# One buffer set for weight blocks and left sums in the first MLP product, with the next pair's blocks asked for at the pair's begin

## The chip, the cores and the metric

The kernel runs on one core of one Trainium2 chip. The metric is device time in microseconds (us) for one execution; the number given for the kernel before is the median of three runs. TensorE is called PE here, VectorE DVE, ScalarE ACT, GpSimd POOL, and SyncE, which only issues DMAs here, SP.

## The reference

The reference is one layer of a streaming encoder on 1024 prompt rows and 64 sample rows: RMSNorm, one input projection, sparse attention and band attention side by side, gates, an output projection and a residual, then an MLP. Only the MLP's first product is touched by the change:

```python
D_MODEL = 1024
SEQ = 1024
DEC_SEQ = 64
D_FF = 4 * D_MODEL

# x: the residual stream, (rows, 1024); w_up (1024, 4096); w_down (4096, 1024)
h = jnp.square(jax.nn.relu(rmsnorm(x, g) @ w_up))
x = x + h @ w_down
```

Rows are 1088 in all, taken as two halves of 544. Everything is float32; a product is made of three matmuls, `hi*hi + hi*lo + lo*hi`, on operands split into a high and a low part.

## The kernel before

The first product, squared ReLU of x times `w_up`, runs over 16 *pairs* of 128 columns of `w_up` (4096 columns in 16 times 256). Each pair is a two-by-two block product done with seven block products in place of eight (Strassen's way, in Winograd's form): the weight blocks are called 11, 12, 21 and 22 (512 x 128 each), the x side was prepared as the split operands T1, T2, T3, T4, B11, B21 and B22, which stay in memory. One block product (`product`) is 24 matmuls 128x272 into two halves of a PSUM tile: 4 slices of the contraction, 2 halves of the rows, 3 matmuls. PE, 24 matmuls at a time, is what the loop is built to feed.

`sums(p)` (L1008) asks for the four blocks of pair p by four DMAs on SP (L1012) and makes four sums of them on DVE: L1014 S1 = 21 + 22, L1015 S3 = 11 - 21 in place, L1016 S2 = S1 - 11 in place, L1017 S4 = 12 - S2 in place. Block 22 stays as it is. `operand` (L1020) splits one such sum: the high part by a copy on ACT (L123), the low part by a subtraction on DVE (L1024). `columns_of` (L647) loads and splits a block of `w_up` that needs no sum (a tile named raw, DMA L652, low part L146). High and low parts live in a ring of five.

The loop `for p in range(NPAIR)` (L1079) does for pair p the products, in program order: T2 with S2 into PSUM tile pf; for the first eight pairs, B11 of pair p + 8 into pa (`first_product`); T1 with S1 into pe; T3 with S3 into pg; for the first eight pairs, B21 of pair p + 8 on top of pa (`second_product`); B22 with S4 on top of pe; T4 with block 22 on top of pg. So pairs 0 to 7 do seven products, and pairs 8 to 15, whose first two were made ahead, do five. Each of pf, pa, pe and pg is one buffer.

DVE reads the PSUM tiles between products: L1087 u from pf; L1096 v from pe after T1 (B22 on pe waits for it); L1103 v from pg after T3 (T4 on pg waits for it); L1109 from pe after B22; L1116 from pg after T4. The results v, u and so on are squared on ACT (L977, L978) and sent out by ACT (L980). Four *left sums* of the results, for the second product, are made on DVE too: L1113 s1, L1118 s2, L1120 in place, L1122 in a12, the block A12 of h that SP reads back from memory (L1100). `sums_out` (L984) sends them out on ACT (L986) one pair later.

All the blocks, the a12 tile and the left sums s1 and s2 are [128, 544] tiles of the pool `up`, by tags: three buffers each for the tags 11, 12, 21 and 22, and two for S1. The a12 tile uses tag 22, s1 uses tag 11 and s2 tag 12. So tag 22's three buffers serve two tiles a pair, block 22 and a12. Before the loop, `quarter(k)` (L1038) prepares a quarter of x's operands with the same tags; its DVE lines are L1044 to L1046 and L1053.

What sets the order: each engine takes its instructions strictly in its own order. A scheduler puts the program's instructions on each engine's queue with the help of simulated times and the program's order as priority; a tile of a pool can be written again when the readers of the buffer's last tile are done. A DMA also waits for the one that used its completion semaphore eight DMAs earlier. In the program, `sums(p + 1)` is called after T1 and L1096 of pair p, `sums_out` after the low part of T1's operand.

Of the kernel before, what the change touches and what calls it, by code (L numbers as in the profile page):

```python
# [10 lines left out]
F32 = mybir.dt.float32  # L11
# [7 lines left out]
P = 128  # L19
# [19 lines left out]
HALF = T // 2  # L39
# [5 lines left out]
def kernel(  # L45
# [8 lines left out]
    nc = tc.nc  # L54
# [26 lines left out]
    def bank(tag, n=512):  # L81
        pool, bufs = banks[tag]
        return pool.tile([P, n], F32, tag=tag, name=tag, bufs=bufs)
# [5 lines left out]
    def open_pool(name, side="left", **reuse):  # L89
        st = ExitStack()  # L90
        p = st.enter_context(tc.tile_pool(name=name, bufs=1, side=side, **reuse))
        pools[name] = st
        return p
# [28 lines left out]
    def copy(out, in_):  # L122
        return nc.scalar.activation(out, in_, AF.Copy)  # L123

    last = {}
# [17 lines left out]
    def split(raw, hi, lo, lo_on_vector=False):  # L143
        copy(hi, raw)
        if lo_on_vector:
            nc.vector.tensor_sub(lo, raw, hi)  # L146
        else:
            nc.gpsimd.tensor_sub(lo, raw, hi)  # L148
# [482 lines left out]
    for g in range(0, EARLY, 4):  # L631
        ws = []
        for k in range(KB):
            raw = pj.tile([P, 512], F32, tag="wraw", name="wraw", bufs=2)
            nc.sync.dma_start(raw, w_in[k * P:(k + 1) * P, C_G + g * P:C_G + g * P + 512])
            hi = pj.tile([P, 512], F32R, tag="whi", name="whi", bufs=11)
            lo = pj.tile([P, 512], F32R, tag="wlo", name="wlo", bufs=11)
# [152 lines left out]
    for mix in "ba":  # L790
        oT[mix] = cp.tile([P, 4, 2, T], F32R, name=f"oT_{mix}")
        for k in range(4):
            for c0, n in CHUNKS:
                raw = cp.tile([P, 384], F32, tag="oraw", name="oraw", bufs=2)[:, :n]
                nc.sync.dma_start(raw, o_dram[mix][k * P:(k + 1) * P, c0:c0 + n])
                hi = oT[mix][:, k, 0, c0:c0 + n]
# [114 lines left out]
    for rows_here in (first_rows, second_rows):  # L911
        for g in range(0, D, 256):
            ws = []
            for k in range(0, KB, 2):
                raw = ring.tile([P, 2, 256], F32, tag="raw", name="raw", bufs=3)
                hi = ring.tile([P, 2, 256], F32R, tag="hi", name="hi", bufs=RING)
                lo = ring.tile([P, 2, 256], F32R, tag="lo", name="lo", bufs=RING)
# [16 lines left out]
    NPAIR = DFF // 256  # L934
# [3 lines left out]
    def product(ps, w, x, opens):  # L938
        for k in range(4):
            for c in range(2):  # L940
                cols = slice(c * HALF // 2, (c + 1) * HALF // 2)
                last = three(ps[:, c * 512:c * 512 + HALF // 2], [(w[k], (xops[x][:, k, 0, cols], xops[x][:, k, 1, cols]))],
                             opens and k == 0, k == 3, not opens)
        return last
# [21 lines left out]
    up = open_pool("up", "right", reuse_waits="tile")  # L966

    def temp(tag, n):
        return hp.tile([P, 2, HALF // 2], F32, tag=tag, name=tag, bufs=n)
# [14 lines left out]
    def sums_out():  # L984
        for p, nm, t in made:
            nc.scalar.dma_start(h_dram[p][BLOCK[nm]][:, :512], t)  # L986
        made.clear()
# [3 lines left out]
    def first_product(p, tag):  # L991
        if p not in begun:
            begin(p, tag)
        ps = begun.pop(p)
        c1 = temp("c1", NEAR + 2)
        copy(c1, halves(ps))
        firsts[p] = ps, c1
# [5 lines left out]
        firsts[p] = c1  # L1003

    def block(nm):
        return up.tile([P, HALF], F32, tag=nm, name=nm, bufs=2 if nm == "s1" else 3)

    def sums(p):  # L1008
        a = {}
        for nm, r, c in (("21", 0, P), ("22", 512, P), ("11", 0, 0), ("12", 512, 0)):  # L1010
            a[nm] = block(nm)[:, :512].rearrange("p (k c) -> p k c", k=4)
            nc.sync.dma_start(a[nm], w_up[r:r + 512, p * 256 + c:p * 256 + c + P].rearrange("(k p) c -> p k c", p=P))  # L1012
        s1 = block("s1")[:, :512].rearrange("p (k c) -> p k c", k=4)
        nc.vector.tensor_add(s1, a["21"], a["22"])  # L1014
        nc.vector.tensor_sub(a["21"], a["11"], a["21"])  # L1015
        nc.vector.tensor_sub(a["11"], s1, a["11"])  # L1016
        nc.vector.tensor_sub(a["12"], a["12"], a["11"])  # L1017
        return {"S1": s1, "S2": a["11"], "S3": a["21"], "S4": a["12"], "A22": a["22"]}

    def operand(src):  # L1020
        hi = ring.tile([P, 4, P], F32R, tag="hi", name="hi", bufs=RING)
        lo = ring.tile([P, 4, P], F32R, tag="lo", name="lo", bufs=RING)
        copy(hi, src)
        last["low"] = nc.vector.tensor_sub(lo, src, hi)  # L1024
        return [(hi[:, k], lo[:, k]) for k in range(4)]

    sources = sums(0)
# [38 lines left out]
    def first_operands():  # L1066
        h, w = (xo.tile([P, 4, 2, HALF], F32R, tag=f"x{nm}_of_x", name=f"first_{nm}", bufs=1) for nm in ("B11", "B21"))
        for k in range(4):
            pair = []
            for t, src, on_vector in ((h, h_dram[k][BLOCK["A11"]][:, :512], True),  # L1070
                                      (w, w_down[k * 256 + P:(k + 1) * 256, :512], True)):
                raw = ring.tile([P, 512], F32, tag="raw", name="raw", bufs=3)
                nc.sync.dma_start(raw, src)
                hi, lo = t[:, k, 0, :512], t[:, k, 1, :512]
                split(raw, hi, lo, lo_on_vector=on_vector)
                pair.append((hi, lo))
            first_ops.append(pair)

    for p in range(NPAIR):  # L1079
        ahead = p + NEAR < NPAIR  # L1080
        if p == NEAR + 2:
            first_operands()
        src = sources
        x6 = bank("pf", 1024)
        product(x6, operand(src["S2"]), "T2", True)
        u = firsts.pop(p)
        nc.vector.tensor_add(u, halves(x6), u)  # L1087
        if ahead:
            first_product(p + NEAR, "pa")
        x5 = bank("pe", 1024)  # L1090
        product(x5, operand(src["S1"]), "T1", True)

        with tc.issue_after(last["low"].ins):
            sums_out()
        v = temp("h", 5)
        nc.vector.tensor_add(v, halves(x5), u)  # L1096
        if p + 1 < NPAIR:
            sources = sums(p + 1)
        a12 = block("22")[:, :512]
        nc.sync.dma_start(a12, h_dram[p][BLOCK["A12"]][:, :512])  # L1100
        x7 = bank("pg", 1024)
        product(x7, operand(src["S3"]), "T3", True)
        nc.vector.tensor_add(v, halves(x7), v)  # L1103
        square_out(p, "A21", v, v)
        if ahead:
            second_product(p + NEAR)
        product(x5, operand(src["S4"]), "B22", False)
        w = temp("h", 5)
        nc.vector.tensor_add(w, halves(x5), u)  # L1109
        square_out(p, "A22", w, w)  # L1110
        a11, a21, a22 = (flat_of(t)[:, :512] for t in (u, v, w))
        s1, s2 = block("11")[:, :512], block("12")[:, :512]
        nc.vector.tensor_add(s1, a21, a22)  # L1113
        made.append((p, "S1", s1))
        product(x7, operand(src["A22"]), "T4", False)
        nc.vector.tensor_add(u, halves(x7), u)  # L1116
        square_out(p, "A11", u, u)
        nc.vector.tensor_sub(s2, s1, a11)  # L1118
        made.append((p, "S2", s2))
        nc.vector.tensor_sub(a21, a11, a21)  # L1120
        made.append((p, "S3", a21))
        nc.vector.tensor_sub(a12, a12, s2)  # L1122
        made.append((p, "S4", a12))
# [117 lines left out]
    for g in range(QUAD):  # L1241
        few = few_operands(g)
        for nm in ("P1", "P2", "P5", "P6", "P3", "P7", "P4"):
# [13 lines left out]
            for k in range(4):  # L1257
                p = 4 * g + k
# [75 lines left out]
```

## Time and profile before

| | |
|---|---|
| median of 3 runs | 1754.68 us (1754.44 to 1754.83) |
| the profiled execution's own time | 1754.13 us |
| its span, first to last instruction | 1752.0 us |
| mean granted clock of PE | 0.995 of full |
| PE busy | 1715.1 us, 98% of the span |
| DVE / ACT / POOL busy | 1200.9 / 957.5 / 478.9 us |
| first MLP product (pairs 0 to 15) | from 1104.94 to 1409.32 us of the span |

The profile is one execution. Its views give, for any stretch, how long each engine was busy, what each idle stretch before an instruction was waiting for, and when each instruction began. A wait is put down to the releaser that came last. PE's matmuls overlap, so PE's busy share says little of small losses; the time from one product's first matmul to the next one's says more.

### The profile page before, as it was taken

To read this page: it belongs to the slowest core of one execution; us is meant where nothing else is said; L and a number is where in the kernel's file an instruction comes from. 1 tells how busy PE (TensorE), PEld (TensorE's weight loads), DVE (VectorE), ACT (ScalarE), POOL (GpSimd) and SP (SyncE) were. 2 spreads that over 40 slices of the span, in tenths; PEclk is the share of its full clock that TensorE was granted. 3 is DMA by queue.
4 is the path that set the end of the run, shared out by engine and by line. 5 is a ranking of instruction groups with operands and counts; after the bars stand their busy time and mean duration, and the time that the engine had idled before them with its cause. 6 is when DMAs were issued, how large, how long until landed. Compare 5 with 4: busy or idle time off the path is not lost.

```text
span 1752.0 us, 30862 instructions
## 1 busy us (share of the span) xinstructions
PE 1715.1 (98%) x10540; PEld 1554.2 (89%) x10540; DVE 1200.9 (69%) x2765; ACT 957.5 (55%) x1994; POOL 478.9 (27%) x549
## 2 busy tenths in 40 slices
PE   8999999999999999999999999999999999999999
PEld 6877888877999999999999999999989988888887
DVE  6877799994457777774354446855577758878787
ACT  5785889722357777775443346644444446443430
POOL 2252432544423333332343444000000011310122
PEclk9999999999999999999999999999999999999999
DMA  5032475454667876654544458654566589665643
GB/s 177 5 89 102 144 200 152 144 167 152 179 165 195 194 170 160 164 133 145 170 141 147 168 173 270 203 169 152 171 198 200 169 282 317 191 205 145 199 126 102
DMA packets 277197, 294.97 MB, mean 168 GB/s; under 512 B 39792, under 2 KB 201584, under 8 KB 277040
## 3 DMA queue, kind: packets, MB, share of 16 engines
q1 hardware_dynamic: 248064, 257.61, 50.7%
q10 hardware_dynamic: 28976, 35.40, 5.7%
q8 instruction: 83, 1.36, 0.3%
q14 instruction: 74, 0.61, 0.1%
HBM read 199.85 MB, written 93.08 MB: 167 GB/s over the span
## 4 chain that ended last, share of the span: by engine, by line
PE 66%; DVE 6%; DMA 4%; issue 2%; ACT 2%; POOL 1%; ACTq 0%; SPq 0%; DVEq 0%; POOLq 0%
PE acc L154 7%; PE acc L156 7%; PE acc L155 7%; PE x L156 5%; PE x L155 5%; PE x L154 5%; PE pt L699 4%; PE po L715 2%; PE s L162 2%; PE po L714 2%; PE s L163 2%; PE few L1253 1%; PE pe L155 1%; PE pe L154 1%; PE pe L156 1%
## 5 line engine op out<-in xcount | busy, mean ns | idle before, releaser
L155 PE MATMUL x<-lo,hi 128*128 128x512 f32 x432 | 168.6, 390 | 0.7 <-POOL lo L148 0.7
L156 PE MATMUL x<-hi,lo 128*128 128x512 f32 x432 | 166.8, 391 | 0.0
L154 PE MATMUL x<-hi 128*128 128x512 f32 x432 | 164.2, 392 | 0.0
L148 POOL TENSOR_TENSOR lo<-wr,hi 128x512 fp32r<-128x512 f32 x15 | 34.5, 2300 | 467.3 <-ACT hi L123 467.3
L148 POOL TENSOR_TENSOR lo<-raw,hi 128x512 fp32r<-128x512 f32 x88 | 117.4, 1344 | 156.8 <-ACT hi L123 156.1
L123 ACT ACTIVATE hi<-raw 128x512 fp32r<-128x512 f32 x104 | 64.2, 626 | 90.5 <-PE acc L155 21.1
L711 DVE TENSOR_TENSOR pl<-pt,ph 128x512 fp32r<-128x512 f32 (+4 forms) x184 | 96.6, 545 | 19.5 <-ACT ph L123 18.9
L536 ACT ACTIVATE nth<-work,cand 128x768 bf16<-128x768 f32 (+2 forms) x93 | 96.6, 1038 | 20.6 <-DVE cand L553 15.3
L146 DVE TENSOR_TENSOR lo<-hr,hi 128x512 fp32r<-128x512 f32 x108 | 81.6, 757 | 27.4 <-ACT hi L123 27.1
L123 ACT ACTIVATE ph<-pt 128x512 fp32r<-128x512 f32 (+4 forms) x184 | 81.6, 483 | 32.5 <-PE pt L699 25.6
L155 PEld LDWEIGHTS x<-lo,hi 128*128 128x128 f32 x432 | 81.1, 188 | 19.2 <-POOL lo L148 1.1
L156 PEld LDWEIGHTS x<-hi,lo 128*128 128x128 f32 x432 | 81.1, 188 | 17.9
L154 PEld LDWEIGHTS x<-hi 128*128 128x128 f32 x432 | 81.1, 188 | 17.5
L154 PE MATMUL acc<-xnT,hi 128*128 128x384 f32 (+1 forms) x288 | 95.4, 331 | 0.0
L156 PE MATMUL acc<-xnT,lo 128*128 128x384 f32 (+1 forms) x288 | 94.3, 327 | 0.0
L155 PE MATMUL acc<-xnT,hi 128*128 128x384 f32 (+1 forms) x288 | 94.3, 327 | 0.0
L686 POOL TENSOR_SCALAR mw<-mw,sm 128x640 f32<-128x640 f32 (+1 forms) x64 | 56.7, 886 | 131.9 <-DVE sm L685 131.8
L154 PE MATMUL wide<-whi,xnT 128*128 128x512 f32 x224 | 89.5, 405 | 1.7 <-DVE work_s L366 1.7
L156 PE MATMUL wide<-whi,xnT 128*128 128x512 f32 x224 | 90.2, 403 | 0.0
L155 PE MATMUL wide<-wlo,xnT 128*128 128x512 f32 x224 | 89.8, 401 | 0.0
L714 PE MATMUL po<-ph,vhl 128*128 128x256 f32 (+2 forms) x336 | 86.0, 274 | 0.4 <-ACT ph L123 0.4
L715 PE MATMUL po<-pl,vhl 128*128 128x256 f32 (+2 forms) x336 | 85.9, 286 | 0.6 <-DVE pl L711 0.6
(671 smaller groups left out, 5973.7 us busy)
## 6 DMA issues: line engine op xcount, KB each, us to landing
hr<-h SPq DMA_DIRECT2D x108, 256.0 KB, 3.7
wr<-in_w_down_dram SPq DMA_DIRECT2D x76, 256.0 KB, 4.0
wraw<-in_w_in_dram SPq DMA_DIRECT2D x56, 256.0 KB, 2.9
h<-h ACTq DMA_DIRECT2D x32, 272.0 KB, 3.1
raw<-in_w_out_dram SPq DMA_DIRECT2D x32, 256.0 KB, 3.1
raw<-in_w_up_dram SPq DMA_DIRECT2D x32, 256.0 KB, 3.7
out_dram<-t SPq DMA_DIRECT2D x24, 256.0 KB, 2.4
g_dram<-gate SPq DMA_DIRECT2D x32, 192.0 KB, 3.4
```

Source lines behind the costliest of these rows:

```text
L123: return nc.scalar.activation(out, in_, AF.Copy)
L146: nc.vector.tensor_sub(lo, raw, hi)
L148: nc.gpsimd.tensor_sub(lo, raw, hi)
L154: nc.tensor.matmul(out, sh, mh, start=(opens and i == 0), stop=False, skip_group_check=resumes)
L155: nc.tensor.matmul(out, sh, ml, start=False, stop=False, skip_group_check=resumes)
L156: last = nc.tensor.matmul(out, sl, mh, start=False, stop=(closes and i == n - 1), skip_group_check=resumes)
L536: nc.scalar.activation(sign[:, :w.shape[1]], w, AF.Sign, bias=against, scale=-1.0, accum_out=col(cnt, j))
L686: nc.gpsimd.tensor_scalar(m[:rows, :n], m[:rows, :n], sm[:rows, 6:7], 1.0, op0=ALU.mult, op1=ALU.mult)
L699: nc.tensor.transpose(ps[:krows, oo:oo + qrows], m[:qrows, kc:kc + krows], ident[:qrows, :qrows])
L711: nc.vector.tensor_sub(pl[:kr, a:b], ps[:kr, a:b], ph[:kr, a:b])
L714: nc.tensor.matmul(dst, vhl[:krows, vt, :], ph[:krows, oo:oo + width], start=(idx == 0), stop=False)
L715: nc.tensor.matmul(dst, vhl[:krows, vt, :], pl[:krows, oo:oo + width], start=False, stop=(idx == n - 1))
```

## The change

`block` now gives all its tiles from one tag, "block", with 14 buffers, as many as the five tags had together; a12, s1 and s2 come from there too. `sums(p + 1)`, with its four DMAs on SP and its four sums on DVE, is called at pair p's begin, ahead of T2's product, in place of after L1096. The low part of `operand` goes through `split`, the same two instructions under another line number (L146 in place of L1024), and `sums_out()` is no longer told to come behind the low part of T1's operand. The number of matmuls, DMAs and bytes is the same.

```diff
     def block(nm):
-        return up.tile([P, HALF], F32, tag=nm, name=nm, bufs=2 if nm == "s1" else 3)
+        return up.tile([P, HALF], F32, tag="block", name=nm, bufs=14)
...
     def operand(src):
         hi = ring.tile([P, 4, P], F32R, tag="hi", name="hi", bufs=RING)
         lo = ring.tile([P, 4, P], F32R, tag="lo", name="lo", bufs=RING)
-        copy(hi, src)
-        last["low"] = nc.vector.tensor_sub(lo, src, hi)
+        split(src, hi, lo, lo_on_vector=True)
...
         src = sources
+        if p + 1 < NPAIR:
+            sources = sums(p + 1)
         x6 = bank("pf", 1024)
         product(x6, operand(src["S2"]), "T2", True)
...
-        with tc.issue_after(last["low"].ins):
-            sums_out()
+        sums_out()
         v = temp("h", 5)
         nc.vector.tensor_add(v, halves(x5), u)
-        if p + 1 < NPAIR:
-            sources = sums(p + 1)
-        a12 = block("22")[:, :512]
+        a12 = block("a12")[:, :512]
         nc.sync.dma_start(a12, h_dram[p][BLOCK["A12"]][:, :512])
```

Line numbers behind the change shift a little: L1087 becomes L1088, L1100 L1098, L1103 L1101, L1109 L1107, L1113 L1111, L1116 L1114, L1118 L1116, L1120 L1118 and L1122 L1120; L1012 to L1017 and L1096 stay.

DVE's order in pair 3, from u of the pair to v's second sum. Before (the numbers in the names count tiles: 12_15052 and 22_15048 are pair 3's sums, 11_15301 and 12_15303 pair 4's, 21_15548, 22_15550 and s1_15556 pair 5's):

```order
L1087 TENSOR_TENSOR c1_13990<-pf_15199,c1_13990 128x544
L1122 TENSOR_TENSOR 22_15059<-22_15059,12_15162 128x512
L1024 TENSOR_TENSOR lo_15380<-12_15052,hi_15379 128x512
L1017 TENSOR_TENSOR 12_15303<-12_15303,11_15301 128x512
L1024 TENSOR_TENSOR lo_15416<-22_15048,hi_15415 128x512
L1096 TENSOR_TENSOR h_15295<-pe_15262,c1_13990 128x544
L1024 TENSOR_TENSOR lo_15452<-11_15301,hi_15451 128x512
L1014 TENSOR_TENSOR s1_15556<-21_15548,22_15550 128x512
L1103 TENSOR_TENSOR h_15295<-pg_15312,h_15295 128x544
```

The same stretch of DVE now (12_14954 and 22_14950 are pair 3's, the names from 15199 to 15207 pair 4's):

```order
L1088 TENSOR_TENSOR c1_13990<-pf_15212,c1_13990 128x544
L1120 TENSOR_TENSOR a12_15059<-a12_15059,12_15162 128x512
L1014 TENSOR_TENSOR s1_15207<-21_15199,22_15201 128x512
L1015 TENSOR_TENSOR 21_15199<-11_15203,21_15199 128x512
L146 TENSOR_TENSOR lo_15380<-12_14954,hi_15379 128x512
L146 TENSOR_TENSOR lo_15416<-22_14950,hi_15415 128x512
L1016 TENSOR_TENSOR 11_15203<-s1_15207,11_15203 128x512
L1096 TENSOR_TENSOR h_15308<-pe_15275,c1_13990 128x544
L1017 TENSOR_TENSOR 12_15205<-12_15205,11_15203 128x512
L146 TENSOR_TENSOR lo_15465<-11_15203,hi_15464 128x512
L1101 TENSOR_TENSOR h_15308<-pg_15312,h_15308 128x544
```

L1014, for pair 5, stood directly ahead of the row that frees pg. Now all four sums in the stretch are pair 4's, and seven rows stand between L1014 and that row.

SP's order in the early pairs, where each row asks for a tile (raw is a block for B11 or B21, the second number of a name ahead of `<-` again a tile's). Before, in pairs 3 and 4 (22_15550, 11_15552 and 12_15554 are pair 5's, 21_16050 is pair 7's):

```order
L1100 DMA 22_15310<-h3_79 128x512
L1012 DMA 22_15550<-in_w_up_dram 128x4x128
L652 DMA raw_15847<-in_w_up_dram 128x4x128
L1012 DMA 21_16050<-in_w_up_dram 128x4x128
L1012 DMA 11_15552<-in_w_up_dram 128x4x128
L1012 DMA 12_15554<-in_w_up_dram 128x4x128
```

Now, in pair 3 (the names from 15199 to 15205 are pair 4's):

```order
L652 DMA raw_15745<-in_w_up_dram 128x4x128
L1012 DMA 21_15199<-in_w_up_dram 128x4x128
L1012 DMA 22_15201<-in_w_up_dram 128x4x128
L1012 DMA 11_15203<-in_w_up_dram 128x4x128
L1012 DMA 12_15205<-in_w_up_dram 128x4x128
L1098 DMA a12_15310<-h3_79 128x512
```

The four blocks of a pair now stand together, ahead of a12, for the pair that comes next. Before, they were asked for apart and two to four pairs ahead, and block 22 stood behind a12.

DVE's order in the late pairs, here the rows between u and v's second sum of pair 10 before (16927, 16925 and s1_16929 are pair 11's):

```order
L1087 TENSOR_TENSOR c1_15009<-pf_16856,c1_15009 128x544
L1024 TENSOR_TENSOR lo_17042<-11_16925,hi_17041 128x512
L1118 TENSOR_TENSOR 12_16785<-11_16784,c1_14758 128x512
L1120 TENSOR_TENSOR h_16701<-c1_14758,h_16701 128x512
L1096 TENSOR_TENSOR h_16919<-pe_16886,c1_15009 128x544
L1122 TENSOR_TENSOR 22_16716<-22_16716,12_16785 128x512
L1024 TENSOR_TENSOR lo_17072<-s1_16929,hi_17071 128x512
L1017 TENSOR_TENSOR 12_16927<-12_16927,11_16925 128x512
L1103 TENSOR_TENSOR h_16919<-pg_16936,h_16919 128x544
```

and of the same pair now (16856 to 16864 are pair 11's):

```order
L1088 TENSOR_TENSOR c1_15022<-pf_16869,c1_15022 128x544
L1120 TENSOR_TENSOR a12_16716<-a12_16716,12_16785 128x512
L1096 TENSOR_TENSOR h_16932<-pe_16899,c1_15022 128x544
L1014 TENSOR_TENSOR s1_16864<-21_16856,22_16858 128x512
L1015 TENSOR_TENSOR 21_16856<-11_16860,21_16856 128x512
L1016 TENSOR_TENSOR 11_16860<-s1_16864,11_16860 128x512
L1101 TENSOR_TENSOR h_16932<-pg_16936,h_16932 128x544
```

Here three sums of the next pair (L1014 to L1016) have come between v's two sums. PE's order in these pairs changes with it: before, a first part of the next pair's T2 stood ahead of B22 or T4 of a pair; now a pair's five products stand one behind the other.

## Rows read from the trace of the kernel before

**Rows 1.** The page's first part: busy us, share of the span, instructions.

```profile
PE 1715.1 (98%) x10540; PEld 1554.2 (89%) x10540; DVE 1200.9 (69%) x2765; ACT 957.5 (55%) x1994; POOL 478.9 (27%) x549
```

**Rows 2.** Stretches: from:to, length, busy us by engine, granted clock, DMA share, GB/s.

```profile
1104.94:1128.40 23.46, 21.62 (x170) 21.18 (x169) 17.53 (x28) 14.11 (x24) 0.00 (x0) 1.00 0.51 156
1128.40:1149.46 21.06, 21.06 (x171) 21.06 (x169) 11.55 (x20) 8.64 (x15) 0.00 (x0) 1.00 0.53 168
1149.46:1170.51 21.05, 21.05 (x170) 21.05 (x169) 12.66 (x20) 9.11 (x16) 0.00 (x0) 1.00 0.54 174
1170.51:1283.57 113.06, 107.16 (x843) 105.64 (x842) 64.26 (x101) 48.72 (x82) 0.00 (x0) 1.00 0.53 170
1283.57:1299.50 15.93, 13.05 (x91) 12.64 (x90) 14.16 (x23) 9.08 (x17) 0.00 (x0) 0.90 0.68 222
1299.50:1409.30 109.80, 109.80 (x873) 109.80 (x872) 76.40 (x122) 48.52 (x78) 0.00 (x0) 1.00 0.55 176
```

**Rows 3.** PE's waits, 1100 to 1412 us: who waited for whom, total, times, longest.

```profile
PE pg L154 <- DVE h L1103: 4.5, 5, 1.7
PE pf L156 <- DVE lo L1024: 1.8, 1, 1.8
...
PE pa L154 <- ACT c L123: 1.4, 1, 1.4
PE pf L154 <- ACT hi L123: 1.1, 1, 1.1
```

**Rows 4.** PE's timeline, pair 3: start, length, what, [idle before, releaser].

```profile
1188.43 0.29 PE L156 MATMUL pe<-xB_of_x,lo 128*128 128x272 f32 x1
1189.37 0.39 PE L154 MATMUL pg<-xT_of_x,hi 128*128 128x272 f32 x1 [0.65 <-DVE h L1103]
```

**Rows 5.** DVE's timeline in the same place.

```profile
1183.34 0.68 DVE L1024 TENSOR_TENSOR lo<-11_15301,hi 128x512 fp32r<-128x512 f32 x1
1187.99 0.69 DVE L1014 TENSOR_TENSOR s<-21_15548,22_15550 128x512 f32<-128x512 f32 x1 [3.97 <-DMA 22_15550<-in_w_up_dram]
1188.60 0.72 DVE L1103 TENSOR_TENSOR h<-pg,h 128x544 f32<-128x544 f32 x1
```

**Rows 6.** SP's timeline in the same place.

```profile
1183.77 0.37 SPq L1012 DMA_DIRECT2D 22_15550<-in_w_up_dram  x1
```

**Rows 7.** SP's waits, 1100 to 1412 us, columns as in rows 3.

```profile
SPq L1012 <- DVE lo L1024: 51.5, 14, 6.3
```

**Rows 8.** DMAs by tile, 1180 to 1300 us: queue, count, KB, us to landing.

```profile
22_15550<-in_w_up_dram SPq DMA_DIRECT2D x1, 256.0 KB, 4.1
...
11_15803<-in_w_up_dram SPq DMA_DIRECT2D x1, 256.0 KB, 6.1
12_15805<-in_w_up_dram SPq DMA_DIRECT2D x1, 256.0 KB, 7.0
22_16052<-in_w_up_dram SPq DMA_DIRECT2D x1, 256.0 KB, 2.9
```

**Rows 9.** Timelines of DVE, ACT and PE in pair 5.

```profile
1222.98 0.69 DVE L1015 TENSOR_TENSOR 21_15799<-11_15803,21_15799 128x512 f32<-128x512 f32 x1 [4.64 <-DMA 11_15803<-in_w_up_dram]
...
1226.24 0.33 ACTq L986 DMA_DIRECT2D h<-h  x1
...
1227.80 0.39 PE L154 MATMUL pa<-xB_of_x,hi 128*128 128x272 f32 x1 [1.36 <-ACT c L123]
```

**Rows 10.** PE's timeline at the seam of pairs 8 and 9.

```profile
1296.13 0.44 PE L156 MATMUL pf<-xT_of_x,lo 128*128 128x272 f32 x1 [1.83 <-DVE lo L1024]
...
1299.77 0.29 PE L154 MATMUL pe<-xB_of_x,hi 128*128 128x272 f32 x1
```

**Rows 11.** DVE's timeline in a late pair.

```profile
1303.78 0.69 DVE L1014 TENSOR_TENSOR s<-21_16703,22_16705 128x512 f32<-128x512 f32 x1 [4.03 <-DMA 22_16705<-in_w_up_dram]
```

**Rows 12.** Timelines of DVE and PE at the loop's start.

```profile
1107.71 0.71 DVE L1046 TENSOR_TENSOR 22_14425<-22_14425,11_14421 128x544 f32<-128x544 f32 x1
...
1109.17 0.39 PE L154 MATMUL pf<-xT_of_x,hi 128*128 128x272 f32 x1 [1.79 <-ACT xT_of_x L123]
```

## The prediction, made before the changed kernel was run

> **What bounds the kernel now.** I began with the page: PE is busy 98% of the span [rows 1], so a faster DVE or DMA gives nothing by itself; only places count where PE itself stands still. Next I cut the changed loop into stretches, at the first matmul of a pair's T2 [rows 2]. Pairs 1 and 2 take 21.06 and 21.05 us and PE's busy time fills them: 168 matmuls in 21.055 us, 0.1253 us each, is what a pair costs that never waits. The reader is to set the other rows against that. Pair 0 took 23.46 us, 2.4 us too much. Pairs 3 to 7 took 113.06 us where 5 x 21.055 = 105.28 would do: 7.8 us too much. In the late part, the 90 matmuls from 1283.57 to 1299.77 [rows 2, 10] took 16.20 us in place of 90 x 0.1253 = 11.28: 4.9 us too much. The rest, 1299.50 to 1409.30, is full. So 7.8 + 4.9 = 12.7 us are lost in the loop behind pair 0, and 2.4 in pair 0. No more than about 15 us can be had here.
>
> The third view is PE's waits over the loop [rows 3]. The commonest by far is T4's first matmul, which waits for DVE's second sum of v (L1103, which frees pg): 5 times, 4.5 us, once in each of pairs 3 to 7. Three single waits follow: a copy of pa on ACT (1.4), a high part on ACT (1.1) and a low part on DVE (1.8). The timelines tell what stands behind each. In pair 3, DVE ended a low part at about 1184.0 and stood still for 3.97 us until block 22 of pair 5 had landed, since L1014 is next in its order; L1103, whose input had long been there, came only at 1188.60 [rows 5], and PE lost 0.65 us at T4 [rows 4]. A wait costs PE more than it shows: from 1188.43 to 1189.37 are 0.94 us between two starts that would be 0.13 apart, and the first matmul behind a wait takes 0.39 in place of 0.29. With both, pair 3's price is some 0.9 us.
>
> Why was block 22 late? SP asked for it at 1183.77 [rows 6] and it took 4.1 us [rows 8]. SP had waited for a low part on DVE that frees a buffer: 51.5 us over 14 such requests [rows 7]. So the chain is a loop: tag 22's three buffers serve block 22 and a12, the load is asked for when DVE has read the old tile, and DVE then waits for the load with PE's release behind it. The wait for pa in pair 5 is the same kind one step on: DVE stood 4.64 us for block 11, so the left sums of the pair before came late; ACT's issue of the one from L1120 went out only at 1226.24, and the copy of pa behind it on ACT let PE go at 1227.80, 1.36 us late [rows 9].
>
> In the seam of pairs 8 and 9 two waits follow one another, the second 1.83 us at 1296.13. Behind it PE's granted clock falls: 0.90 over that stretch, 1.00 in all others [rows 2]. From 1296.13 to 1299.77 are 16 matmuls in 3.64 us, where 2.0 would do, at starts 0.23 apart, about the lower of the two levels, 1.2 GHz. So 1.6 of the 4.9 us is the clock's.
>
> **The change part by part.** *One tag with 14 buffers.* The memory is the same, and so is the number of DMAs and matmuls; what goes is the rule that block 22 and a12 share three buffers. A pair uses eight tiles (four blocks, S1, a12, s1, s2), so 14 buffers are 1.75 pairs' worth. The instructions cost what they cost. The gain is the lost time that hangs on late blocks.
>
> *Loads and sums at the pair's begin.* Per pair, SP issues four loads for the next pair one behind the other, each 0.37 us [rows 6], ahead of a12. By my following of the semaphores, the second raw load ahead of them waits for DVE at the end of the pair before, so the four are asked for between 1.5 and 5 us into the pair; the last, block 12, waits for a left sum's output. They land between 4.5 and 12 us into it, by landings of 2.9 (alone) to 7.0 us (fourth in a row) [rows 8]. In pairs 1 to 7 L1014 and L1015 therefore still wait on DVE, about to +5.5 and +8 us, and perhaps L1017 up to +12. But what stands behind them has time: pg is full at 4 x 3.01 = 12.0 us (T2, B11, T1, T3), T4 begins at 6 x 3.01 = 18.1 us, and L1101 is 0.72 us long [rows 5]. Between them lie 6.0 us of B21 and B22, which hide a wait of up to some 5 us. The other waiter, B22 at 15.1 us, needs L1096 and one low part, both behind L1015 only; 7 us of cover. So I cost the waits that stay at nothing; if a load came at +18, the price would be that of before, 0.4 to 1.7 us a pair [rows 3]. The seven pairs' 7.8 us go. The left sums now stand ahead of L1014 on DVE, so the wait for pa in pair 5, which is part of these 7.8, goes too.
>
> *The late pairs.* In pairs 8 to 15 all loads can be asked for a pair ahead, since only half as many raw loads stand on SP. What is worse there: T2 of the next pair no longer stands ahead of T4, and L1101 has only B22's 3.0 us between the end of T3 (+9.0) and the start of T4 (+12.1). L1096 can start at T1's end (+6.0); behind it L1014, L1015 and L1016 take three times 0.61 (pitch from L1014 to L1103 [rows 5]) and end at about +8.7, before T3 does. L1101 then runs from +9.1 to +9.8: 2.3 us to spare. DVE was busy 76.40 of 109.80 us in the late pairs [rows 2], 70%, and its work there stays the same. So no wait is added and the 4.9 us of the seam go, with the clock's 1.6 among them, since the clock fell only behind those waits.
>
> *Low part's line, sums_out.* The same instructions; 0 us. ACT's order of outputs moves a little; ACT was busy 48.72 of 113.06 us [rows 2], and an output issue that waits on ACT is priced by the pair-5 wait, 1.4 us at most, once.
>
> *The loop's start.* Here L1014 of pair 1 comes two rows ahead of L1046 of the last quarter, and PE's 1.79 us wait in pair 0's T2 hangs on L1046 by way of an ACT copy [rows 12]. One more row of 0.61 us on that chain: +0.6. Ends: -2.4 (the shared tag asks for the quarter's tiles earlier and pair 0 loses nothing), and +4.0 if L1014 has to wait there as long as it did in a late pair, 4.03 us [rows 11]. I take +0.6, because block 22 is asked for some 4 us before L1014's turn, which is about the longest landing of that block that is shown [rows 8].
>
> *A remainder.* A new order of some 500 instructions on DVE and ACT [rows 2] will have some wait that I did not find; from 0 to 3.7 us (1.05 + 1.83 and their restarts, the largest that stood in one place). I take one like pair 3's, 0.9 us.
>
> Sum: -7.8 - 4.9 + 0.6 + 0.9 = -11.2 us. From the profiled execution's 1754.13 that is 1742.9; it lies 0.55 us under the median of 1754.68, so against the median 1743.5.
>
> **The rule that speaks against it.** PE's T4 wait comes five times in a row, pair by pair [rows 3]. The Trainium skill, page "Perfetto Trace Analysis", section "Identifying Performance Opportunities", says that the same gap repeating on the engine that should be full can mean that there is not enough memory for the next tile (buffer count, tile sizes). By that rule a change that adds no buffer leaves the gap, and the time would be 1754.7. The rows point at the division, not the total: SP waited for one tag while 11 other buffers of the pool were not asked. I weigh it as the third rival.
>
> **The rivals.**
> 1. *The wait moves but half of it stays.* Pairs 1 to 7 ask for blocks only in the pair before their use; if block 12 lands beyond +16 or so, T4 or the next T2's operand (S2, which needs L1016) waits. For it: landings of 6 to 7 us when several are asked for in a row [rows 8]. Against: 5 to 6 us of cover. Price: half of 7.8 stays and a start worse by 2, about 1748 (1746 to 1751). On this bears the Trainium skill, "DMA: Bandwidth & Descriptors", section "Issuing engines are not separate DMA queues": transfers run on the same 16 engines and interleave, whoever starts them. The trace agrees, 2.9 us for a load alone and 7.0 for the fourth in a row; by it block 12 comes at +12 and not at +8, still inside the cover.
> 2. *Slower: the late pairs lose their cover.* If L1014 of a late pair waits 4.03 us as it once did [rows 11], from +6.7 on, L1016 ends at +12.5 and L1101 at +13.3 in place of at most 12.0; T4 is 1.3 us late and restarts, 1.6 us, in each of eight pairs: 13 us. It decides from the point where block 22 lands later than about +9 us in the pair in which it is summed. With the start's worst (+4), the time is 1743.5 + 13 + 3 = 1759 (1758.2 to 1762); alone it gives 1756. Against: these loads are asked for a pair ahead.
> 3. *It doesn't do what it says.* The shared set comes free no earlier, because a12, s1 and s2 hold their buffers until their outputs have landed; the same waits come back, about 1754 (1751.2 to 1758.2).
>
> **How the numbers follow.** A measurement of this kernel can tell about 0.2%, 3.5 us. Forecast (1739.5 to 1746): 0.56. Rival 1 (1746 to 1751): 0.18. Rival 3 with the mild form of rival 2: 0.14. Rival 2 in full: 0.12. The likeliest gives 1743.5. Below the forecast lies only the start's gain, 1754.7 - 12.7 - 2.4 = 1739.6. The upper end takes in rival 1 and the upper edge of the unknown start, and a little of rival 3: 1752.5. Outside are about 0.2. Faster by over 0.2% (under 1751.2): 0.74; within: 0.14; slower: 0.12.
>
> **What would show it.** Right: the stretches of pairs 1 to 7 are all 21.06 us long; no wait of PE for L1101 is left; the granted clock is 1.00 at pairs 8 and 9; DVE still shows waits of L1014 and L1015 for blocks in pairs 1 to 7, harmless. Rival 1: T4 or T2 waits in the pairs from 1 to 7 behind L1017 or a low part. Rival 2: T4 waits for L1101 eight times from pair 8 on, each behind a DMA. Rival 3: SP's waits for DVE in L1012 as long as before. Wrong at the start: pair 0's stretch over 24.1 us. The whole argument falls if the time changes outside the stretch from some 1080 us to the loop's end.

## The result

The changed kernel took 1738.4 us (median of 6 runs, 1736.8 to 1742.7), the kernel before beside it 1754.5 us (6 runs, 1752.9 to 1754.8): a ratio of 0.9913, 95% interval 0.9901 to 0.9926, so 0.74 to 0.99% faster. The forecast was 1743.5 us with a range from 1739.5 to 1752.5; the time lies 1.1 us below the range.

The page of the changed kernel, first part, to be set against [rows 1]; its span is 1738.0 us, the execution's own time 1739.8 us:

```profile
PE 1709.3 (98%) x10540; PEld 1551.3 (89%) x10540; DVE 1199.3 (69%) x2765; ACT 956.4 (55%) x1994; POOL 481.4 (28%) x549
```

No engine got less work: the instructions are as many, DVE's, ACT's and POOL's busy times differ by 1.1 to 2.5 us, and PE's is 5.8 us lower. The stretches of the loop, cut as in [rows 2], tell where the time went (length, busy us of PE, weight loads, DVE, ACT and POOL, granted clock, DMA share, GB/s):

```profile
1102.98:1125.43 22.45, 21.51 (x170) 21.16 (x169) 15.85 (x26) 13.37 (x23) 0.00 (x0) 1.00 0.32 101
1125.43:1146.48 21.05, 21.05 (x170) 21.05 (x169) 12.81 (x21) 9.84 (x16) 0.00 (x0) 1.00 0.54 178
1146.48:1167.54 21.06, 21.06 (x171) 21.06 (x169) 12.91 (x21) 9.63 (x16) 0.00 (x0) 1.00 0.55 179
1167.54:1272.81 105.27, 105.27 (x843) 105.27 (x842) 66.40 (x105) 50.36 (x85) 0.00 (x0) 1.00 0.56 184
1272.81:1287.87 15.06, 15.06 (x122) 15.06 (x121) 12.92 (x21) 8.48 (x15) 0.00 (x0) 1.00 0.88 282
1287.87:1393.37 105.50, 105.50 (x843) 105.50 (x842) 76.76 (x120) 44.52 (x73) 0.00 (x0) 1.00 0.56 180
```

From pair 1 on PE's busy time fills every row, and the clock is 1.00 in the seam of pairs 8 and 9, where it was 0.90. Pairs 3 to 7 take 105.27 us, five times the 21.05 of a pair that never waits; they took 113.06. All waits of PE that are left from 1040 to 1396 us are two, both ahead of pair 0's end; compare [rows 3]:

```profile
PE pg L154 <- ACT c L123: 1.5, 1, 1.5
PE pf L154 <- ACT xT_of_x L123: 0.9, 1, 0.9
```

DVE in pair 5 of the changed kernel, which answers to [rows 5] and [rows 9], shows that it still waits for its blocks (start, length, what, idle time before it and its releaser):

```profile
1218.67 0.69 DVE L1014 TENSOR_TENSOR s<-21_15701,22_15703 128x512 f32<-128x512 f32 x1 [4.15 <-DMA 22_15703<-in_w_up_dram]
1220.49 0.69 DVE L1015 TENSOR_TENSOR 21_15701<-11_15705,21_15701 128x512 f32<-128x512 f32 x1 [1.13 <-DMA 11_15705<-in_w_up_dram]
...
1224.74 0.71 DVE L1101 TENSOR_TENSOR h<-pg,h 128x544 f32<-128x544 f32 x1
```

And PE at the same place:

```profile
1227.56 0.29 PE L156 MATMUL pe<-xB_of_x,lo 128*128 128x272 f32 x1
1227.68 0.29 PE L154 MATMUL pg<-xT_of_x,hi 128*128 128x272 f32 x1
```

L1014 stood for 4.15 us, as long as before. But it did so from 4.9 to 9.0 us in a pair of 21, and the row that frees pg ended at 1225.45, 2.2 us before T4 wanted it: the two starts of PE are 0.12 us apart. So the wait was not removed; it was moved to a place where it is hidden.

### The profile page after: what moved, and what is told of

The parts are those of the page before. It is cut to its first block, busy times and chain, and to the rows that moved or that the text cites. A ratio compares the mean times of both kernels' runs of the same rounds, so it can differ in the third digit from the quotient of the medians.

```text
span 1738.0 us, 30914 instructions
## 1 busy us (share of the span) xinstructions
PE 1709.3 (98%) x10540; PEld 1551.3 (89%) x10540; DVE 1199.3 (69%) x2765; ACT 956.4 (55%) x1994; POOL 481.4 (28%) x549
## 4 chain that ended last, share of the span: by engine, by line
PE 85%; DVE 6%; DMA 3%; issue 3%; ACT 2%; POOL 1%; SPq 0%; ACTq 0%; DVEq 0%; POOLq 0%
PE acc L154 9%; PE acc L156 9%; PE acc L155 9%; PE x L156 5%; PE x L155 5%; PE x L154 5%; PE pt L699 4%; PE wide L154 3%; PE wide L155 3%; PE wide L156 3%; PE s L162 3%; PE po L715 2%; PE s L163 2%; PE po L714 2%; PE pg L156 2%
## 5 line engine op out<-in xcount | busy, mean ns | idle before, releaser
L146 DVE TENSOR_TENSOR lo<-hr,hi 128x512 fp32r<-128x512 f32 x108 | 81.6, 756 | 28.9 <-ACT hi L123 28.7
```

## The experiments

Up to the first pf product all kernels of this section run the same instructions in the same order (the part before the loop differs from there on). So the table gives, from each profiled execution, the time from that product to pair 2's T2 ("start"), pairs 2 to 7, pairs 8 to 15 up to the second product ("late"), and their sum; then when the first pf product began and what came behind the loop. All in us, read from PE's timelines.

| kernel | start | pairs 2-7 | late | sum | first pf product | behind |
|---|---|---|---|---|---|---|
| before | 96.15 | 134.11 | 125.75 | 356.01 | 1053.31 | 342.68 |
| e2_early | 95.66 | 132.24 | 126.53 | 354.43 | 1051.94 | 343.23 |
| changed | 95.90 | 126.33 | 120.56 | 342.79 | 1050.58 | 344.63 |
| a0_again | 95.78 | 126.32 | 120.56 | 342.66 | 1051.28 | 342.46 |
| e1_tag | 96.04 | 126.32 | 120.56 | 342.92 | 1051.33 | 343.35 |
| x1_order | 96.79 | 126.32 | 124.96 | 348.07 | 1051.48 | 343.65 |
| e8_a12 | 98.89 | 126.32 | 122.20 | 347.41 | 1051.76 | 342.93 |
| x4_seam | 95.97 | 126.32 | 121.83 | 344.12 | 1050.70 | 343.28 |
| e4_buf9 | 98.45 | 126.32 | 120.56 | 345.33 | 1051.20 | 341.97 |
| e4_buf7 | 106.57 | 126.32 | 120.53 | 353.42 | 1051.08 | 343.40 |
| e9_start | 95.64 | 126.32 | 120.56 | 342.52 | 1051.10 | 343.18 |
| y_late | 95.53 | 126.32 | 121.17 | 343.02 | 1053.30 | 343.08 |
| e10_vec | 92.71 | 126.32 | 120.56 | 339.59 | 1054.02 | 343.19 |
| e11_vec | 92.72 | 126.32 | 120.56 | 339.60 | 1051.61 | 342.69 |

**The two parts apart.** e1_tag is the kernel before with only this:

```diff
-        return up.tile([P, HALF], F32, tag=nm, name=nm, bufs=2 if nm == "s1" else 3)
+        return up.tile([P, HALF], F32, tag="block", name=nm, bufs=14)
```

> One part alone: the kernel before with the one tag of 14 buffers; the call of the next pair's sums stays where it was. Theory A (the division of the buffers into tags set the order, the call's place nothing): the loop from pair 0 to pair 15 has no wait of PE, 290.4 us as in the changed kernel (304.4 before), the time is that of the changed kernel, 1738.4 give or take 1.5. Rival B (the earlier call brings part of it): half of the loop's 14 us stay, 1745 to 1748.

Measured: 1738.9 us against 1751.5 before on its chip, ratio 0.9932 (0.9920 to 0.9945), sum of the stretches 342.92. e2_early is the other part alone:

```diff
         src = sources
+        if p + 1 < NPAIR:
+            sources = sums(p + 1)
...
-        if p + 1 < NPAIR:
-            sources = sums(p + 1)
         a12 = block("22")[:, :512]
```

> The other part alone: the kernel before, its tags as they were, with the next pair's sums called at the pair's begin. Theory A: every engine's order comes out as before, so 1754.5 give or take 1, with the same waits of T4 for L1103's kin (4.5 us in 5). Rival B: 1746 to 1750. Whatever this run differs from the kernel before by is chance, since the two programs hold the same instructions in the same order.

Measured: 1751.9 us, ratio 1.0005 (0.9996 to 1.0015), PE's T4 waits are there (2.9 us in 4), sum 354.43. The tag did all of it. The earlier call in the program, which the change's name speaks of, moves next to nothing: built alone it gives every engine the order of before, but for two neighbours on ACT in a late pair that change places, and the tag alone gives the order of the changed kernel on every engine. At both places of the call the blocks were asked for in the same order, so here the buffers set it. The two also show what chance does: 1.6 us between two executions of the same loop (356.01 and 354.43).

**Order or buffers.** x1_order keeps the tags and forces one row:

```diff
-        nc.vector.tensor_add(s1, a["21"], a["22"])
+        if "v" in last:
+            with tc.issue_after(last["v"].ins):
+                nc.vector.tensor_add(s1, a["21"], a["22"])
+        else:
+            nc.vector.tensor_add(s1, a["21"], a["22"])
...
-        nc.vector.tensor_add(v, halves(x7), v)
+        last["v"] = nc.vector.tensor_add(v, halves(x7), v)
```

> The kernel before, tags and call as they were, with one thing forced: L1014 of the pair ahead comes behind the second sum of v (L1103) on DVE and not directly ahead of it. Theory A, its mechanism (DVE stands at L1014 for block 22 while the row that frees pg waits behind it): the five waits of T4 go, 4.5 us and some 2 of restarts, and the pa wait, the seam of pairs 8 and 9 (4.9) and the start stay: 1747 to 1749. Rival C (PE would wait anyway, since DVE is behind with its work): 1753 to 1757.

Measured: 1742.7 us, 0.9956 (0.9943 to 0.9970). Pairs 2 to 7 take 126.32, so the five T4 waits are gone and the pa wait of pair 5 with them, which had not been expected; with it, and with 1751.5 us for the kernel before beside this run, the time lies under the expected 1747 to 1749. DVE in pair 3 (its L1107 is L1103, its L1016 is L1014):

```profile
1181.55 0.72 DVE L1107 TENSOR_TENSOR h<-pg,h 128x544 f32<-128x544 f32 x1 [1.53 <-PE pg L156]
1182.92 0.69 DVE L1016 TENSOR_TENSOR s<-21_15548,22_15550 128x512 f32<-128x512 f32 x1 [0.65 <-DMA 22_15550<-in_w_up_dram]
```

DVE now waits for PE at the row that frees pg, and not the other way round. Of PE's waits from 1100 to 1400 us these stay, the seam of pairs 8 and 9 (1.8 and 0.3) and pair 0:

```profile
PE pf L156 <- DVE lo L1028: 1.8, 1, 1.8
PE pf L154 <- ACT xT_of_x L123: 1.8, 1, 1.8
PE pf L154 <- ACT hi L123: 0.3, 1, 0.3
```

So one row on DVE was worth the 7.8 us of pairs 1 to 7. e8_a12 goes at the same wait from the buffers' side:

```diff
-        return up.tile([P, HALF], F32, tag=nm, name=nm, bufs=2 if nm == "s1" else 3)
+        return up.tile([P, HALF], F32, tag=nm, name=nm, bufs={"s1": 2, "22": 2, "a12": 1}.get(nm, 3))
...
-        a12 = block("22")[:, :512]
+        a12 = block("a12")[:, :512]
```

> The kernel before with the three buffers of tag 22 divided: two for block 22, one of its own for a12; 14 in all. Theory D (block 22 is late because a12 sits in its buffers): L1014's waits of 2.6 to 4.4 us shrink below 1 us and the pg waits go, 1746 to 1749. Theory A (it is the fixed division by tag as such; two buffers for block 22 tie its load to the use of the block two pairs back just as well): L1014 stands ahead of the second sum of v as before and waits as before, 1752 to 1758.

Measured: 1743.0 us, 0.9957 (0.9943 to 0.9971). Theory A of that expectation was wrong here. L1014 still stands directly ahead of L1103, and PE's waits are gone from pairs 2 to 7; L1014's own waits shrank in these pairs to 0.7 to 1.8 us, most of them not below 1 as theory D had it, and PE was not kept waiting by them. DVE and SP in pair 3:

```profile
1184.42 0.69 DVE L1014 TENSOR_TENSOR s<-21_15548,22_15550 128x512 f32<-128x512 f32 x1 [1.66 <-DMA 22_15550<-in_w_up_dram]
1185.03 0.72 DVE L1103 TENSOR_TENSOR h<-pg,h 128x544 f32<-128x544 f32 x1
```

```profile
1181.56 0.37 SPq L1012 DMA_DIRECT2D 22_15550<-in_w_up_dram  x1
1182.35 0.34 SPq L1100 DMA_DIRECT2D a<-h  x1
```

Block 22 goes out ahead of a12 now, 2.9 us before L1014 runs; before, 4.2 us lay between ([rows 5, 6]), and L1014 waited 3.97 us and not 1.66. So the harm needed both: a load that comes late because a12 sits in its buffers, and a row that waits for it ahead of the one that PE wants. Either one taken away is enough, for pairs 2 to 7. At the start e8_a12 is 3.0 us longer than the changed kernel: T2 waits 3.3 us there for x's quarters, perhaps because tag 22 has one buffer less for them; that was not tried.

**The seam.** x4_seam is x1_order with the second product's first operands held back:

```diff
-        if p == NEAR + 2:
-            first_operands()
+        if p == NEAR + 3:
+            with tc.issue_after(last["v"].ins):
+                first_operands()
```

> The kernel before with L1014 forced behind the second sum of v (as in x1_order) and, besides, the second product's first operands (eight loads on SP, eight splits) held back behind pair 10. Theory S1 (the seam's waits come from these loads and splits standing ahead of block 11 and S2's low part): the late stretch falls from 125.0 to some 120.6 us and the time by 4.4, 1738 to 1740. Theory S2 (block 11 is late because its buffer is tied to tag 11 and the left sum s1): the late stretch stays at 124 to 126, 1742 to 1744.

Measured: 1741.2 us, 0.9942 (0.9929 to 0.9956); the late stretch is 121.83, 3.1 us less than in x1_order. The wait for S2's low part is gone; one wait of 0.8 us (B22 for v's first sum) came in. So the seam was mostly those eight loads and splits, in the way of block 11 and S2. They need not be moved for that: the changed kernel keeps them where they were and has no wait there, and e8_a12 keeps them too and lost only 1.6 us in the late part (122.20). The medians of x4_seam and x1_order, 1.5 us apart, don't tell them apart by themselves; the stretches do.

**How many buffers.** The changed kernel with bufs=9:

> The changed kernel with 9 buffers in the one tag in place of 14. Theory A (the common set counts, not its size): the order of the loop stays, no wait of PE in it, changed stretch 342 to 344 us, time as with 14 buffers, 1738 to 1740. Rival E (a set of 14 gives the loads their lead of a pair; 9 is hardly more than the eight tiles of one pair): SP waits for buffers, L1014 waits longer and T4 waits come back, 1743 to 1755.

Measured: 1740.7 us, 0.9940 (0.9927 to 0.9954); no wait behind pair 0, late 120.56. What it lost, 2.6 us, it lost at the start, where x's quarters use the same set; so the sum of 345.33 and the time are a little over what was expected. And with bufs=7:

> The changed kernel with 7 buffers in the one tag, fewer than the eight tiles of one pair. Theory A (PE waits as soon as DVE stands for a block that was asked for late ahead of the row that frees pg, or of S2): SP now has to wait for buffers of the same pair, the blocks of a late pair land at 9 us or later, and T4 or T2 begin late in most of the pairs 8 to 15, where 2.1 us are to spare: 1 to 4 us each, changed stretch 352 to 375 us, 1748 to 1771. If the early ask is not needed for that, 343 to 346 us and 1739 to 1741 as with 9.

Measured: 1750.7 us, 1.0000 (0.9989 to 1.0011). The time was as expected, its place was not: pairs 2 to 7 and the late pairs are full (126.32 and 120.53), and 10.7 us are lost at the start, 8.5 of them in pair 1 of the loop; most of PE's waits there are for x's operands. From pair 2 on 7 shared buffers do what 14 divided ones did not.

**The cover of the late pairs.** y_late was to hold the late loads back and to put all four sums ahead of the second sum of v:

```diff
+        if NEAR <= p < NPAIR - 1:
+            with tc.issue_after(first.ins):
+                sources = sums(p + 1)
...
+        if NEAR <= p < NPAIR - 1:
+            with tc.issue_after(last["sum"].ins):
+                nc.vector.tensor_add(v, halves(x7), v)
```

> The changed kernel with the cover of pairs 8 to 14 taken away: the next pair's four loads are held back behind L1096 of the pair, and the second sum of v behind the four sums that use them. Theory A (PE waits as soon as DVE stands for a block ahead of the row that frees pg; in the changed kernel that row has 2.1 us to spare): the loads are asked for at 6.8 to 8.3 us in the pair, land at 10.5 to 13.3, and T4 or the first matmuls of T2 begin 2 to 3.5 us late in each of seven pairs: 14 to 26 us, 1753 to 1765. If PE is not bound there, 1738 to 1742.

Measured: 1739.9 us, 0.9932 (0.9919 to 0.9946). It did not make what it was to make: the order on DVE came out as written, but the loads were not held back. SP asked for them ahead of the row they were to follow (pair 11's four blocks at 1299.96 to 1308.25 us, L1096 of pair 10 at 1312.01), since the hold sets only the order on an engine's own queue. So the price of a late load in the late pairs was not tried. The run does show the placement by itself, in pair 10:

```profile
1314.83 0.69 DVE L1017 TENSOR_TENSOR 12_16927<-12_16927,11_16925 128x512 f32<-128x512 f32 x1
1315.44 0.72 DVE L1106 TENSOR_TENSOR h<-pg,h 128x544 f32<-128x544 f32 x1
```

and PE:

```profile
1318.09 0.29 PE L154 MATMUL pg<-xT_of_x,hi 128*128 128x272 f32 x1
```

DVE's row (its L1106) ends at 1316.16, and T4 begins at 1318.09: 1.9 us to spare behind four sums whose blocks had landed. Only pair 8 had a late block (1.55 us at L1017), and there T4 was 0.2 us late.

**The start.** e9_start holds L1014 of pair 1 behind the last quarter's L1045:

> The changed kernel with L1014 of pair 1 held behind the last quarter's difference (L1045), so that the chain to PE's wait in pair 0's T2 is one row of DVE shorter. If that row is on the path, the 0.9 us wait there shrinks to 0.3 and the stretch from the first pf product to pair 1 from 74.9 to 74.3 us; the time is 0.6 lower, too little to be seen in the medians. If the chain is bound by ACT's copies, nothing moves.

Measured: 1738.6 us, 0.9925 (0.9914 to 0.9937), start 95.64; the wait is 0.9 us as before. That row was not on the path. DVE's rows there told of something else; the changed kernel:

```profile
1089.35 0.72 DVE L146 TENSOR_TENSOR xT_of_x<-12_14386,xT_of_x 128x544 fp32r<-128x544 f32 x1
1089.99 1.82 DVE L1045 TENSOR_TENSOR 22_14388<-22_14388,11_14384 128x544 f32<-128x544 f32 x1
1091.73 1.81 DVE L1043 TENSOR_TENSOR 11_14406<-12_14408,11_14406 128x544 f32<-128x544 f32 x1
1093.46 0.71 DVE L1052 TENSOR_TENSOR 21_14390<-21_14390,22_14388 128x544 f32<-128x544 f32 x1
```

and its POOL:

```profile
1089.33 1.90 POOL L148 TENSOR_TENSOR lo<-raw,hi 128x512 fp32r<-128x512 f32 x1 [3.78 <-PE pf L155]
1091.45 1.51 POOL L148 TENSOR_TENSOR lo<-raw,hi 128x512 fp32r<-128x512 f32 x1 [0.23 <-ACT hi L123]
```

Two subtractions on DVE, begun while POOL does one, take 1.8 us in place of 0.7; the row at 1089.35, begun with POOL's, takes 0.72. Both long rows end 0.58 us behind the end of POOL's row, and POOL's rows are longer too, 1.5 and 1.9 us where they take 1.3 with DVE out of the way: it looks as if the two engines took turns, which these rows suggest and no run tests. Between the first pf product and pair 1 there are four such long rows of DVE. e11_vec is e9_start with the last of POOL's low parts before the loop taken to DVE:

```diff
-            product(begun[p], columns_of(w_up, 0, 0, p * 256, p >= NEAR), "B11", True)
+            product(begun[p], columns_of(w_up, 0, 0, p * 256, p >= NEAR - 3), "B11", True)
...
-        product(ps, columns_of(w_up, 0, 1, p * 256, p >= NEAR), "B21", False)
+        product(ps, columns_of(w_up, 0, 1, p * 256, p >= NEAR - 3), "B21", False)
```

> The changed kernel with L1014 of pair 1 held behind the last quarter's difference (as in e9_start) and the low parts of the last three B11 and B21 blocks before the loop taken from POOL to DVE. If POOL's rows are what makes some DVE rows take 1.82 in place of 0.71 us there, three or more slow rows of 1.1 us go and six rows of 0.6 us come: the stretch from the first pf product to pair 1 stays at 74 to 75 us, 1738 to 1739. If DVE's slow rows stay, the stretch grows by up to 3.6 us: 1740 to 1742.

Measured: 1735.7 us, 0.9917 (0.9904 to 0.9931), start 92.72. The gain, 3.2 us against the changed kernel and 2.9 against e9_start, was more than expected: of the four slow rows one is left (1.78 us), and both waits of PE have gone. e10_vec has that edit on the changed kernel, without e9_start's; a0_again is the changed kernel on the same chip.

> The changed kernel with only the low parts of the last three B11 and B21 blocks before the loop taken from POOL to DVE, L1014 of pair 1 where the change left it. If the slow DVE rows beside POOL made the 3.2 us that e11_vec saved at the start, the stretch from the first pf product to pair 1 is 71.7 to 72.5 us, against 74.9 in the changed kernel, and the time 3 us under that of a0_again; if L1014's place made it, 74 to 75 us and no difference.

> The changed kernel itself once more, on the chip that times the next run: its changed stretch from the first pf product to the second product is 342.8 us give or take 0.4, its median 1737 to 1740; against the kernel before -11 to -14 us, since the stretches with unchanged code differ by chance from one execution to the next.

Measured: e10_vec 1736.4 us, 0.9912 (0.9897 to 0.9927); a0_again 1738.4 us, 0.9927 (0.9914 to 0.9940); before, beside them, 1750.5. Start 92.71 against 95.78. So POOL's rows made the start's waits, and L1014's place none of them. The edit takes away two things at once, POOL's own longer rows and the slow rows of DVE beside them; which of the two PE waited for was not tried apart. The stretch from the first pf product to pair 1 of e10_vec has no idle time of PE at all:

```profile
1054.02:1125.68 71.66, 71.66 (x579) 71.56 (x578) 51.70 (x81) 48.23 (x87) 9.81 (x8) 1.00 0.76 234
```

By stretches e10_vec is 3.1 us better than the changed kernel (339.59 and 342.66); by medians 2.0 us, with intervals that overlap.

## Why the prediction was right and where it missed

**Pairs 1 to 7, -7.8 us: right.** They took 155.17 us and take 147.38 (1125.43 to 1272.81): 7.8 us, all of it in pairs 3 to 7. The mechanism, DVE standing for a late block ahead of the row that PE wants, was tested from both sides (x1_order, e8_a12). What I had credited to the loads and sums at the pair's begin is the tag's: e1_tag has it all, e2_early none. L1014's and L1015's waits stayed, as foreseen, and were hidden. The cover was smaller than I gave it: not 5 to 6 us but 2.2 (pair 5) to 4.2 (pair 1), because I put the end of DVE's wait at +8 us in the pair; in pair 5 L1015 ran at +10.9. Loads asked for together took longer than I had from [rows 8]. The 7.0 us there is not a fourth load in a row, as I read it, but the third: before, SP asked for 21, 11 and 12 together and for block 22 some ten us ahead of them. In pairs 1 to 7 of the changed kernel block 22, second in a row, landed after 4.6 to 6.4 us, block 11 after 5.7 to 7.7 and block 12 after 6.1 to 8.3, the longest each time in pair 5:

```profile
21_15701<-in_w_up_dram SPq DMA_DIRECT2D x1, 256.0 KB, 5.8
22_15703<-in_w_up_dram SPq DMA_DIRECT2D x1, 256.0 KB, 6.4
11_15705<-in_w_up_dram SPq DMA_DIRECT2D x1, 256.0 KB, 7.7
12_15707<-in_w_up_dram SPq DMA_DIRECT2D x1, 256.0 KB, 8.3
```

Here the rule of the Trainium skill that was weighed in rival 1 (page "DMA: Bandwidth & Descriptors", section "Issuing engines are not separate DMA queues", transfers on the same 16 engines interleave) has the trace with it: even the first of the four took 5.8 us, where a load alone took 2.9. The delay stayed inside the cover.

**Late pairs, -4.9 us: right in kind, a little small.** 125.75 against 120.56, 5.2 us. The 0.3 us that I missed lay in the rest that I had called full: its 870 matmuls took 109.55 us (1299.77 to 1409.32), and 109.26 at the pace of the changed kernel's late pairs. The slack of the second sum of v was worked out as 2.3 us and is 2.1 in every one of the eight pairs; pair 10:

```profile
1311.28 0.69 DVE L1016 TENSOR_TENSOR 11_16860<-s,11_16860 128x512 f32<-128x512 f32 x1
1312.20 0.72 DVE L1101 TENSOR_TENSOR h<-pg,h 128x544 f32<-128x544 f32 x1 [0.24 <-PE pg L156]
...
1315.02 0.29 PE L154 MATMUL pg<-xT_of_x,hi 128*128 128x272 f32 x1
```

**The start, +0.6 us: wrong sign, small.** From the first pf product to pair 1 it took 75.09 us and takes 74.85, so -0.2: the wait of [rows 12] fell from 1.8 to 0.9 us, and one for an ACT copy ahead of it, in a product on pg, rose from 0.5 to 1.5. I had put L1014's 0.61 us on the path to the 1.79 us wait of [rows 12]. e9_start shows that it was not there; POOL's rows and DVE's slow rows beside them were (e10_vec), and I had not read them.

**The remainder, +0.9 us: wrong.** No new wait came behind the start: 0.

With these four terms as measured the loop's sum is -13.2 us in this pair of executions and not -11.2; by repeats of both orders (356.01 and 354.43; 342.79, 342.66 and 342.92) it is -12.4.

**The base: the step that failed.** The mechanism was right and the terms of the loop nearly so; what put the time below the range is the number that they were taken from. The sum was taken from one execution's 1754.13 us and the median of three, 1754.68, as if they were exact, and the lower end of the range, 1754.7 - 12.7 - 2.4, left no room for an error in them. Both were high for this kernel. In the four later comparisons the kernel before had medians of 1750.5 to 1751.7 us (17, 11, 15 and 11 runs, 1745.1 to 1755.7 in all), while the changed program, by its own name and as e1_tag, stayed at 1738.4 to 1738.9. So 1751 less 12.4 gives 1738.6, what was measured; 1754.7 less 11.2 gave 1743.5. Some 3.7 us of the 5.1 that the forecast was off are the base, the rest the start, the remainder and the late pairs. Against the kernel before on the same chip the changed program saved 12.1 and 12.6 us in the later comparisons; the 16.2 of the first has an interval of 13 to 17. The loop can hardly have given 16.2, since by the prediction's own count PE had lost 15.1 us there (12.7 + 2.4); in the profiled pair, 14.0 us apart by their spans, 13.2 are the loop's and 0.8 those of the unchanged stretches.

Why the base was high stays open. The first pf product, with only unchanged instructions ahead of it, began between 1050.58 and 1054.02 us in fourteen executions, half of them before 1051.4, and the execution that I read began it at 1053.31. Behind the loop the spread is 342.0 to 344.6, and there that execution was among the short ones (342.7). Both together took 1396.0 us in it and 1394.7 in the middle of the fourteen, so this explains 1.3 us; its loop took 1.6 us more than that of e2_early. Chance from one execution to the next is hardly all: of the 54 later executions of the kernel before 12 took 1752.9 us or more, and in the first comparison all six did. The prediction's sign that the argument falls, a change outside the stretch from some 1080 us to the loop's end, did come in the profiled pair, 2.7 us less ahead of the first pf product and 2.0 more behind the loop; since the instructions there are the same and other executions spread as wide, it speaks against the base and not against the mechanism.

**The rivals.** Rival 1 (half of the waits stay) and rival 2 (the late pairs lose their cover) did not come; rival 2's price stays untested, since y_late did not make its late load. Rival 3, that a common set without more bytes changes nothing, is refuted by e1_tag, and by e4_buf9 and e4_buf7: even fewer buffers keep the loop free of waits from pair 2 on. The rule of the Trainium skill that stood beside it (page "Perfetto Trace Analysis", section "Identifying Performance Opportunities", a repeating gap can mean too little memory) does not describe this loop: the gap repeated, the memory was enough, and its division was the cause. At the start memory does count: with 7 buffers it lost 10.7 us.

## What to carry to other kernels

A wait on a side engine costs by what stands behind it in that engine's order, so look which row the bound engine needs next and how long the rows ahead of it can stand; here the same 4 us of DVE waiting cost up to 1.7 us a pair in one place and nothing in another. Where tiles that live differently long share a few buffers by name, as block 22 and a12 did, try a common set of the same size; here it took nothing but a tag. And before a small effect is subtracted from a base, see how far the base itself moves between executions.

## What the runs showed that was not expected

The subtraction of 128x544 on DVE took 0.71 us alone and 1.82 us when begun during POOL's own subtraction of 128x512, and each of the four long rows of the start ended 0.6 us behind the end of POOL's; with six such POOL rows (1.3 to 1.9 us) done on DVE instead, the start became 3.1 us shorter, though DVE had six rows more to do. And stretches with the same instructions differ by up to 3.4 us between executions (the 1050 us up to the first pf product), while pairs that never wait repeat to 0.02 us over 126.
